# A two-layer hybrid block: attention scores of two heads at a time, the low-key part in the upper and lower half of the array

## The chip, the core and the metric

One core of a Trainium2 chip runs the whole program. Its tensor engine (PE) multiplies a stationary tile of weights (up to 128 rows by 128 columns) with a moving tile of up to 512 columns and adds into PSUM; the vector engine (DVE), the scalar engine (ACT) and GpSimd (POOL) do the rest, and sixteen DMA engines move data. Each engine works through its own instructions in the order in which they stand. The metric is the device time in microseconds, as the median of the runs.

## The reference, cut to what matters

Two layers of a hybrid backbone work on 512 latent tokens and 256 context tokens, 1024 channels wide. One input projection feeds four mixers: A global attention, W windowed attention, a spatial gating, an mLSTM; gates, a merge and an output projection follow. Both attentions have 8 query heads on 2 key/value heads, 64 channels a head. What the change touches is this part:

```python
def attend_dense(q, k, v):                                   # A: all 768 keys for a latent query
    s = jnp.einsum('bqhgd,bkhd->bhgqk', q, k).astype(jnp.float32) * HEAD_DIM ** -0.5
    p = jax.nn.softmax(s, axis=-1).astype(v.dtype)
    return jnp.einsum('bhgqk,bkhd->bqhgd', p, v)
...
    s_ctx = jnp.einsum('bqhgd,bkhd->bhgqk', qb, kc) * scale   # W: 256 context keys,
    s_loc = jnp.einsum('bqhgd,bkhd->bhgqk', qb, kb) * scale   # and the keys within 128 positions
    s_loc = jnp.where(ok, s_loc, -jnp.inf)
    p = sink_softmax(jnp.concatenate([s_ctx, s_loc], axis=-1))
```

Context queries read only the 256 context keys, and only in the first layer.

## The kernel before, in words

Tokens lie in six tiles of 128: tiles 0 to 3 latent, 4 and 5 context. Nearly all products are made on a type that PE runs at one pass (fp32r); for precision an operand is split into a high and a low part, and a product of two split operands is made of three: high by high, high by low, low by high. These are the helper's products on line 244 (`mm`), and most of PE's work is such projections into the PSUM tiles named `d`. Transposes, and a few products in the gate arithmetic, run in plain float32.

For the attention a query head has 64 channels, so its high and low part fit together: `rotate` (line 543 on) lays a query head down as 64 high and 64 low channels, and each key head twice, once as high, high and once as low, low. `turn` (line 574) transposes these with PE, so that the parts lie along the array's 128 rows: high in the upper 64 rows, low in the lower. A pass of a query tile over the doubled high keys is thus (high + low) by high, and one over the doubled low keys (high + low) by low, both with 128 rows.

`attend_scores` takes one head and a pair of query tiles. For each tile it fills one PSUM buffer `s` (there are two) with the scores, in pieces of 512, 256 or 128 keys, each piece in two passes; DVE adds masks and finds the maximum, ACT makes the exponential with its sum. `attend_values` transposes the probabilities of the pair (line 858), ACT and DVE split them (lines 861 and 862), and PE multiplies them with the split values into the buffer `b`; the high and low halves are added at the end (lines 874 and 876). In the windowed attention the two tiles of a pair share most of their keys; a key tile that only one of them sees gives a product of 128 columns.

What sets the order: the attention, the gate arithmetic and the mLSTM form one generator (`mixers`), the input projections another (`fill`). `interleave` hands out steps of the two by credit: a step of attention is worth its estimated time by a factor `RATIO`, one factor for each layer and phase, and steps of projections are drawn as long as there is credit. `FILL_ORDER` lists the projection units; a unit named t is an early merge gate, which otherwise is computed in the merge. Steps of `mixers` have a higher priority, and the framework's scheduler then orders each engine's instructions by a modelled time, so an instruction whose buffer isn't free in the model is passed over for one that can go.

Of the kernel before, what the change touches and what calls it, by code (L numbers as in the profile page):

```python
# [10 lines left out]
F32R = mybir.dt.float32r  # L11
AF = mybir.ActivationFunctionType
# [7 lines left out]
XT = 4  # L20
# [8 lines left out]
def _in_units():  # L29
# [27 lines left out]

OFF = 250
PP_FROM = 3
RATIO = ((1.5, 1.3, 1.5), (1.2, 0.4, 1.5))  # L60
N2, N3 = 1, 1
LEAD = (4,6)
LAG = 26.0
# [3 lines left out]
SIDE_K = 1  # L67
AFTER = {(0, 6): "g_v0", (0, 7): "g_v1", (2, 0): "g_u0", (2, 3): "g_u1"}
FILL_ORDER = (
    "w_kv w_q0 gate0_0 m0 m1 a_q1 m2 m3 m_o0 gate0_1 w_q1 t0_2 m4 gate1_0 t2_3 gate1_1 gate2_0 t3_3 t0_0 t2_0 gate2_1 t1_1 t1_0 gate3_0 m_o1 m5 t0_3 t1_3 t2_1 t0_1 t3_1 gate3_1 t1_2",  # L70
    "a_q1 m0 w_kv gate0_0 w_q0 m1 m2 g_v0 m3 w_q1 t1_1 m4 m_o0 gate0_1 t1_2 g_v1 t3_0 t0_2 m_o1 gate1_0 m5 t2_2 t0_3 g_u0 g_u1 gate1_1 t3_2 t2_0 gate2_0 gate2_1 t3_3 gate3_0 t3_1 gate3_1 t0_1 t1_3")
FIRST1 = (("kv", 4), ("x", 1), ("q", 2), ("x", 1), ("kv", 9), ("w", 1), ("q", 9))
FIRST0 = (("kv", 3), ("q", 3), ("kv", 9), ("w", 1), ("q", 9))
# [8 lines left out]
def tile_hybrid_block(ctx, tc, A, out):  # L82
# [16 lines left out]
    def S():  # L99
        return ps_s.tile([128, 1024], F32, tag="s", name="s")  # L100
# [142 lines left out]
    def mm(o, l, r, start, stop):  # L243
        pe.matmul(o, l, r, start=start, stop=stop)  # L244
# [307 lines left out]
    def rotate(ear, nh, t, g, tabs, copies):  # L552

        e, a, r = ear
        shape = [128, nh, 64]
        ev, av = (z.rearrange("p (h d) -> p h d", h=nh) for z in (e, a))
        if r is not None:
            dve.tensor_mul(ev, ev, bc(r.rearrange("p (h o) -> p h o", o=1), shape))
        if t < XT:
            dve.tensor_mul(av, ev, bc(tabs[0][:, t:t + 1, :], shape))  # L560
            dve.tensor_mul(ev, ev, bc(tabs[1][:, t:t + 1, :], shape))
            dve.tensor_add(av[:, :, 0:32], av[:, :, 0:32], ev[:, :, 32:64])
            dve.tensor_add(av[:, :, 32:64], av[:, :, 32:64], ev[:, :, 0:32])
            ev, e = av, a
        elif g is not None:
            dve.tensor_mul(ev, ev, bc(g.rearrange("p (o d) -> p o d", o=1), shape))
        st = ST()
        sv = st.rearrange("p (h s d) -> p h s d", h=nh, s=2 * copies)
        f = e.rearrange("p (h o d) -> p h o d", h=nh, o=1).to_broadcast([128, nh, copies, 64])
        act.copy(sv[:, :, 0:copies, :].bitcast(F32R), f)  # L570
        dve.tensor_sub(sv[:, :, copies:, :].bitcast(F32R), f, sv[:, :, 0:copies, :])
        return st

    def turn(st, dst, mark, done):
# [206 lines left out]
            act.activation(v[:, gs], ps[:, gs], AF.Identity, bias=sgb[:, g:g + 1])  # L781


    def attend_scores(qT, kv, kT, hl, pair, mode, sc, sink, sums):
        is_x = pair[0] < XT
        Ps = []
        for t in pair:
            ps = S()
            qs = qT[:, hl, t * 128:(t + 1) * 128]

            if not is_x:
                pieces = [(0, 512, 256)]
                cols = {4: 0, 5: 128}
                n = 256
            elif mode == "A":
                pieces = [(0, 0, 512), (512, 512, 256)]
                cols = {j: 128 * j for j in range(6)}
                n = 768
            else:
                loc = [j for j in (t - 1, t, t + 1) if 0 <= j < XT]  # L800
                cols = {4: 0, 5: 128}
                for i, j in enumerate(loc):
                    cols[j] = 256 + 128 * i
                pieces = [(0, 512, 256), (256, loc[0] * 128, 256)]
                if len(loc) == 3:
                    pieces.append((512, loc[2] * 128, 128))
                n = 256 + 128 * len(loc)
            for (pc, kc, cn) in pieces:
                mm(ps[:, pc:pc + cn], qs, kT[:, 2 * kv, kc:kc + cn], True, False)
                mm(ps[:, pc:pc + cn], qs, kT[:, 2 * kv + 1, kc:kc + cn], False, True)  # L810
            if is_x and mode == "W":
                if len(loc) == 3:
                    mv = ps[:, 256:768].rearrange("p (a b) -> p a b", a=2)[:, :, 0:128]
                    dve.tensor_add(mv, mv, mask)
                elif loc[0] == t:
                    dve.tensor_add(ps[:, 384:512], ps[:, 384:512], mask[:, 1, :])
                else:
                    dve.tensor_add(ps[:, 256:384], ps[:, 256:384], mask[:, 0, :])
            mx, nm, sm = YX(1), YX(1), sums[:, t:t + 1]
            dve.reduce_max(out=mx, in_=ps[:, :n], axis=AX.X)  # L820
            if sink is None:
                dve.tensor_scalar(nm, mx, -sc, None, op0=ALU.mult)
            else:
                dve.tensor_scalar(nm, mx, -sc, sink[0], op0=ALU.mult, op1=ALU.min)  # L824
            P = M(n)
            act.activation(P, ps[:, :n], AF.Exp, bias=nm[:, 0:1], scale=sc, accum_out=sm)  # L826
            if sink is not None:
                es = YX(1)
                act.activation(es, sink[1], AF.Exp, bias=nm[:, 0:1])
                dve.tensor_add(sm, sm, es)  # L830
            Ps.append((P, cols))
            yield 0.0011 * n
        return Ps

    def attend_values(Ps, Vt, kv, pair, mode, yT, hl):
        is_x = pair[0] < XT

        if not is_x:
            groups = [[(4, 0, 2), (5, 0, 2)]]
        elif mode == "A":  # L840
            groups = [[(j, 0, 2) for j in range(3)], [(j, 0, 2) for j in range(3, 6)]]
        else:
            c0, c1 = Ps[0][1], Ps[1][1]
            both = [j for j in range(XT) if j in c0 and j in c1]
            single = [(j, 0, 1) for j in range(XT) if j in c0 and j not in c1]
            single += [(j, 1, 1) for j in range(XT) if j in c1 and j not in c0]
            groups = [[(4, 0, 2), (5, 0, 2)] + single, [(j, 0, 2) for j in both]]
        pv = B()
        done = 0
        total = sum(len(g) for g in groups)  # L850
        for g in groups:
            n = sum(b[2] for b in g) * 128
            pt = S()
            o = 0
            for (j, q0, nq) in g:
                for qi in range(q0, q0 + nq):
                    P, cols = Ps[qi]
                    pe.transpose(pt[:, o:o + 128], P[:, cols[j]:cols[j] + 128], ident)  # L858
                    o += 128
            ph, pl = M(n, F32R), M(n, F32R)  # L860
            act.copy(ph, pt[:, :n])  # L861
            dve.tensor_sub(pl, pt[:, :n], rd(ph))  # L862
            o = 0
            for (j, q0, nq) in g:
                oc = slice(q0 * 128, (q0 + nq) * 128)
                ic = slice(o, o + nq * 128)
                vs = Vt[:, j, kv, :]
                mm(pv[:, oc], vs, ph[:, ic], done == 0, False)
                done += 1
                mm(pv[:, oc], vs, pl[:, ic], False, done == total)  # L870
                o += nq * 128
            yield 0.0017 * n
        tmp = XS(64)
        act.copy(tmp, pv[64:128, :256])
        o = 64 * (hl % 2)
        dve.tensor_add(yT[o:o + 64, :], pv[:64, :256], tmp)
        yield 0.0

    def attention(l, mode, b, ydram, rsd, res):
        nq = NT if l == 0 else XT  # L880
        sums = G48(8 * nq).rearrange("p (h t) -> p h t", h=8)
        pairs = [(0, 1), (2, 3)] + ([(4, 5)] if l == 0 else [])
        sc = 0.125
        if mode == "W":
            sk = const.tile([128, 16], F32, tag="sink", name="sink")
# [3 lines left out]
        for kv in range(2):  # L889
            yield ("need", (mode, kv))  # L890
            kT, Vt, qs = res[mode]
            for hp in range(2):
                for pair in pairs:
                    yT = XS()
                    for hl in (2 * hp, 2 * hp + 1):
                        h = 4 * kv + hl
                        sink = (sk[:, 8 + h:9 + h], sk[:, h:h + 1]) if mode == "W" else None
                        Ps = yield from attend_scores(qs[kv], kv, kT, hl, pair, mode, sc, sink, sums[:, h, :])
                        if pend is not None:
                            yield from finish_attend(pend, ydram, b, mode)  # L900
                        pend = (Ps, Vt, kv, pair, yT, hl, hp)
            if kv == 1:
                yield from finish_attend(pend, ydram, b, mode)
            release(res, "big", 1 + kv)
            release(res, "v6", kv)

# [8 lines left out]
    def finish_attend(pend, ydram, b, mode):  # L915
        Ps, Vt, kv, pair, yT, hl, hp = pend
        yield from attend_values(Ps, Vt, kv, pair, mode, yT, hl)
        if hl % 2 == 1:
            sy.dma_start(out=ydram[b, 2 * kv + hp][:, pair[0] * 128:pair[0] * 128 + 256], in_=yT)


    KAPPA = 0.25 * 128.0 ** -0.5
# [766 lines left out]
```

## Time and profile before

| | us |
|---|---|
| median of 3 runs | 2027.65 (2026.71 to 2029.03) |
| the profiled execution | 2029.01, of it span of the trace 2027.2 |
| PE busy in the span | 1983.9 |
| DVE, ACT busy | 1314.6, 972.7 |

The clock that TensorE was granted was 0.997 of full over the span. A start in the timeline is that of the operands' stream; the duration beside it is longer than the distance to the next start, since products overlap. So PE's pace is read from starts that follow each other.

### The profile page before, as it was taken

To read this page: it belongs to the slowest core of one execution; us is meant where nothing else is said; L and a number is where in the kernel's file an instruction comes from. 1 tells how busy PE (TensorE), PEld (TensorE's weight loads), DVE (VectorE), ACT (ScalarE), POOL (GpSimd) and SP (SyncE) were. 2 spreads that over 40 slices of the span, in tenths; PEclk is the share of its full clock that TensorE was granted. 3 is DMA by queue.
4 is the path that set the end of the run, shared out by engine and by line. 5 is a ranking of instruction groups with operands and counts; after the bars stand their busy time and mean duration, and the time that the engine had idled before them with its cause. 6 is when DMAs were issued, how large, how long until landed. Compare 5 with 4: busy or idle time off the path is not lost. (4 is left out here: it accounts for less than half of the span.)

```text
span 2027.2 us, 34553 instructions
## 1 busy us (share of the span) xinstructions
PE 1983.9 (98%) x13216; PEld 1805.3 (89%) x13216; DVE 1314.6 (65%) x2859; ACT 972.7 (48%) x2178; POOL 77.9 (4%) x88
## 2 busy tenths in 40 slices
PE   7999999999999999999999989999999999999998
PEld 5998998999999899999988989989989898888788
DVE  5766865676656766667445588667676565456765
ACT  5655554354544544334333466555555465443333
POOL 1200100000000000001000022000000000000000
PEclk9999999999999999999999999999999999999999
DMA  8112233333332544675343342223334335447745
GB/s 306 54 56 79 89 95 120 123 101 120 123 115 95 187 146 165 208 216 163 103 149 122 126 156 76 89 91 115 97 116 138 116 102 168 162 140 231 228 160 182
DMA packets 124271, 274.96 MB, mean 136 GB/s; under 512 B 16033, under 2 KB 41289, under 8 KB 123465
## 3 DMA queue, kind: packets, MB, share of 16 engines
q1 hardware_dynamic: 123560, 272.13, 40.9%
q8 instruction: 104, 1.70, 0.3%
q14 instruction: 63, 0.51, 0.1%
q0 software_dynamic: 256, 0.54, 0.1%
q10 hardware_dynamic: 288, 0.07, 0.0%
HBM read 219.33 MB, written 53.36 MB: 135 GB/s over the span
## 5 line engine op out<-in xcount | busy, mean ns | idle before, releaser
L244 PE MATMUL d<-xh,wh 128*128 128x512 f32 (+1 forms) x1504 | 536.6, 357 | 0.2
L244 PE MATMUL d<-xh,wl 128*128 128x512 f32 (+1 forms) x1504 | 534.4, 355 | 0.0
L244 PE MATMUL d<-xl,wh 128*128 128x512 f32 (+1 forms) x1504 | 533.5, 355 | 0.0
L228 DVE TENSOR_TENSOR wl<-wr,wh 128x1024 fp32r<-128x1024 f32 (+3 forms) x264 | 281.9, 1091 | 59.6 <-ACT wh L227 57.9
L244 PEld LDWEIGHTS d<-xh,wh 128*128 128x128 f32 x1504 | 284.3, 189 | 35.2 <-DVE st L686 0.3
L244 PEld LDWEIGHTS d<-xh,wl 128*128 128x128 f32 x1504 | 284.2, 189 | 34.7
L244 PEld LDWEIGHTS d<-xl,wh 128*128 128x128 f32 x1504 | 284.3, 189 | 33.8
L227 ACT CAST wh<-wr 128x1024 fp32r<-128x1024 f32 (+3 forms) x264 | 238.2, 946 | 138.4 <-PE s L244 52.8
L244 PE MATMUL d<-wh,xh 128*128 128x256 f32 (+1 forms) x976 | 282.8, 291 | 3.6 <-DVE xh L1567 1.9
L244 PE MATMUL d<-wh,xl 128*128 128x256 f32 (+1 forms) x976 | 278.5, 286 | 0.6 <-DVE xl L421 0.5
L244 PE MATMUL d<-wl,xh 128*128 128x256 f32 (+1 forms) x976 | 278.2, 286 | 0.8 <-DVE wl L228 0.8
L244 PEld LDWEIGHTS d<-wh,xh 128*128 128x128 f32 x976 | 186.6, 192 | 8.0 <-issue 4.5
L244 PEld LDWEIGHTS d<-wl,xh 128*128 128x128 f32 x976 | 187.2, 192 | 1.3 <-DVE wl L228 1.0
L244 PEld LDWEIGHTS d<-wh,xl 128*128 128x128 f32 x976 | 186.9, 192 | 1.4 <-DVE xl L421 0.9
L862 DVE TENSOR_TENSOR m<-s,m 128x768 fp32r<-128x768 f32 (+2 forms) x144 | 119.7, 837 | 97.7 <-ACT m L861 97.2
L244 PE MATMUL s<-big,wh 128*128 128x512 f32 (+1 forms) x656 | 163.8, 357 | 6.1 <-ACT big L1384 2.6
L826 ACT ACTIVATE m<-s,yx 128x768 f32<-128x768 f32 (+3 forms) x160 | 120.4, 753 | 96.8 <-DVE yx L824 49.4
L820 DVE TENSOR_REDUCE yx<-s 128x1 f32<-128x768 f32 (+3 forms) x160 | 122.4, 765 | 33.3 <-PE s L244 32.1
L861 ACT CAST m<-s 128x768 fp32r<-128x768 f32 (+2 forms) x144 | 100.9, 706 | 85.5 <-PE s L858 84.4
L244 PE MATMUL b<-m,v 128*128 128x256 f32 (+1 forms) x768 | 131.4, 284 | 2.9 <-DVE m L862 1.8
L244 PEld LDWEIGHTS s<-big,wh 128*128 128x128 f32 x656 | 107.3, 188 | 26.1 <-ACT big L1384 4.7
L244 PE MATMUL s<-big 128*128 128x256 f32 (+2 forms) x680 | 118.9, 302 | 0.7 <-ACT big L578 0.7
(343 smaller groups left out, 3064.6 us busy)
## 6 DMA issues: line engine op xcount, KB each, us to landing
wr<-in_w_in_dram SPq DMA_DIRECT2D x100, 512.0 KB, 4.2
wr<-in_w_mg_dram SPq DMA_DIRECT2D x50, 512.0 KB, 4.6
wr<-in_w_mod_dram SPq DMA_DIRECT2D x32, 512.0 KB, 4.6
wr<-in_w_out_dram SPq DMA_DIRECT2D x32, 512.0 KB, 4.6
th<-st SPq DMA_DIRECT2D x50, 256.0 KB, 2.4
wr<-in_w_bp_dram SPq DMA_DIRECT2D x50, 256.0 KB, 3.6
wr<-in_w_br_dram SPq DMA_DIRECT2D x28, 384.0 KB, 4.0
m<-th SPq DMA_DIRECT2D x26, 384.0 KB, 5.5
```

Of the source, the lines that this page charges most:

```text
L227: act.copy(wh[:, sl], raw)
L228: dve.tensor_sub(wl[:, sl], raw, rd(wh[:, sl]))
L244: pe.matmul(o, l, r, start=start, stop=stop)
L820: dve.reduce_max(out=mx, in_=ps[:, :n], axis=AX.X)
L826: act.activation(P, ps[:, :n], AF.Exp, bias=nm[:, 0:1], scale=sc, accum_out=sm)
L861: act.copy(ph, pt[:, :n])
L862: dve.tensor_sub(pl, pt[:, :n], rd(ph))
```

## The change

Scores are now made for two heads of one query tile, instead of for two tiles of one head. A query head's parts are laid down as high, low for the first head of a pair and low, high for the second, so that the high parts of the two heads lie in different halves of the rows. The pass over the high keys is as before. The pass over the low keys takes the high query part alone, with 64 rows: the first head in the upper half of the array, the second in the lower half, written in turns; low by low is left out. Context tiles keep 128 rows in both passes. The windowed pieces are laid out anew, so that the first is always 512 keys wide. The values follow with the two heads of a tile in 256 columns. Two of the ratios are lower, and the unit t3_2 of the first layer is computed early.

```diff
-RATIO = ((1.5, 1.3, 1.5), (1.2, 0.4, 1.5))
+RATIO = ((1.4, 1.2, 1.5), (1.2, 0.4, 1.5))
...
-    "w_kv w_q0 gate0_0 m0 m1 a_q1 m2 m3 m_o0 gate0_1 w_q1 t0_2 m4 gate1_0 t2_3 gate1_1 gate2_0 t3_3 t0_0 t2_0 gate2_1 t1_1 t1_0 gate3_0 m_o1 m5 t0_3 t1_3 t2_1 t0_1 t3_1 gate3_1 t1_2",
+    "w_kv w_q0 gate0_0 m0 m1 a_q1 m2 m3 m_o0 gate0_1 w_q1 t0_2 m4 gate1_0 t2_3 gate1_1 gate2_0 t3_3 t0_0 t2_0 gate2_1 t1_1 t1_0 gate3_0 m_o1 m5 t0_3 t1_3 t2_1 t0_1 t3_1 gate3_1 t1_2 t3_2",
...
-        sv = st.rearrange("p (h s d) -> p h s d", h=nh, s=2 * copies)
-        f = e.rearrange("p (h o d) -> p h o d", h=nh, o=1).to_broadcast([128, nh, copies, 64])
-        act.copy(sv[:, :, 0:copies, :].bitcast(F32R), f)
-        dve.tensor_sub(sv[:, :, copies:, :].bitcast(F32R), f, sv[:, :, 0:copies, :])
+        sv = st.rearrange("p (a s d) -> p a s d", a=2, s=4)
+        if copies == 2:
+            f = e.rearrange("p (h o d) -> p h o d", h=2, o=1).to_broadcast([128, 2, 2, 64])
+            hi, lo = sv[:, :, 0:2, :], sv[:, :, 2:4, :]
+        else:
+            f = e.rearrange("p (a b d) -> p a b d", a=2, b=2)
+            hi, lo = sv[:, :, 0::3, :], sv[:, :, 1:3, :]
+        act.copy(hi.bitcast(F32R), f)
+        dve.tensor_sub(lo.bitcast(F32R), f, hi)
...
+    def attend_scores(qT, kv, kT, hp, t, mode, sc, sinks, sums):
+        if t >= XT:
+            pieces = [(0, 256, slice(512, 768))]
+            cols = {4: 0, 5: 128}
+        elif mode == "A":
+            pieces = [(0, 512, slice(0, 512)), (512, 256, slice(512, 768))]
+            cols = {j: 128 * j for j in range(6)}
+        else:
+            first = (0, 1) if t < 2 else (2, 3)
+            cols = {first[0]: 0, first[1]: 128, 4: 256, 5: 384}
+            pieces = [(0, 512, None if t < 2 else slice(256, 768))]
+            if t in (1, 2):
+                cols[3 - t] = 512
+                pieces.append((512, 128, slice(384 - 128 * t, 512 - 128 * t)))
...
+        def products(ps, q, rows, kr, first):
+            for (pc, cn, ks) in pieces:
+                out, keys = ps[:, pc:pc + cn], kT[rows, kr, :]
+                if ks is None:
+                    mm(v3(out, 2), q, v3(keys, 3)[:, 0::2, :], first, not first)
+                else:
+                    mm(out, q, keys[:, ks], first, not first)
+                yield
+
+        qs = [qT[:, 2 * hp + i, t * 128:(t + 1) * 128] for i in range(2)]
+        pss = [S(), S()]
+        for i in range(2):
+            for _ in products(pss[i], qs[i], slice(0, 128), 2 * kv, True):
+                pass
+        rows = [slice(0, 128)] * 2 if t >= XT else [slice(0, 64), slice(64, 128)]
+        halves = [products(pss[i], qs[i][rows[i]], rows[i], 2 * kv + 1, False) for i in range(2)]
+        for _ in zip(*halves):
+            pass
...
+            if t < XT and mode == "W":
+                for j in (t - 1, t + 1):
+                    if j in cols and j < XT:
+                        mv = ps[:, cols[j]:cols[j] + 128]
+                        dve.tensor_add(mv, mv, mask[:, int(j > t), :])
...
+        keys = sorted(cols, key=lambda j: cols[j])
+        groups = [keys] if len(keys) == 2 else [keys[:3], keys[3:]]
...
-        o = 64 * (hl % 2)
-        dve.tensor_add(yT[o:o + 64, :], pv[:64, :256], tmp)
+        for i in range(2):
+            cs = slice(128 * i, 128 * i + 128)
+            dve.tensor_add(yT[64 * i:64 * i + 64, o:o + 128], pv[:64, cs], tmp[:, cs])
```

The order of PE's instructions at three places. The names: `s` with a number is a score buffer, so one number is one head and tile; `d` is a projection, `b` the values. First the start of global attention in the first layer, before, where one head and tile fills a buffer (two passes of 512, two of 256):

```order
L244 MATMUL d_1090<-wh_879,xl_129 128x256
L244 MATMUL s_1213<-big_590,big_643 128x512 x2
L244 MATMUL s_1213<-big_590,big_643 128x256 x2
L577 MATMUL d_1115<-ident_98,st_1021 128x128 x4
L244 MATMUL d_1134<-wh_879,xh_128 128x256
```

The same place in the changed program; the last four score products are the two heads' half products:

```order
L244 MATMUL d_1090<-wh_879,xh_128 128x256
L244 MATMUL d_1090<-wl_880,xh_128 128x256
L244 MATMUL s_1213<-big_590,big_643 128x512
L244 MATMUL s_1213<-big_590,big_643 128x256
L244 MATMUL s_1214<-big_590,big_643 128x512
L244 MATMUL s_1214<-big_590,big_643 128x256
L244 MATMUL s_1213<-big_590,big_643 128x512
L244 MATMUL s_1214<-big_590,big_643 128x512
L244 MATMUL s_1213<-big_590,big_643 128x256
L244 MATMUL s_1214<-big_590,big_643 128x256
L582 MATMUL d_1115<-ident_98,st_1021 128x128 x4
```

Here the second head's products have moved up to the first's, and the half products of the two stand in turns. The next query tile, before:

```order
L244 MATMUL d_1173<-wh_879,xh_128 128x256
L244 MATMUL s_1235<-big_590,big_643 128x512 x2
L244 MATMUL s_1235<-big_590,big_643 128x256 x2
L244 MATMUL d_1173<-wl_880,xh_128 128x256
L244 MATMUL d_1173<-wh_879,xl_129 128x256
```

And in the changed program, from the first head's last half products to the second head's:

```order
L244 MATMUL s_1235<-big_590,big_643 128x512
L244 MATMUL s_1235<-big_590,big_643 128x256
L244 MATMUL d_1173<-wl_880,xh_128 128x256
L244 MATMUL d_1173<-wh_879,xl_129 128x256
L244 MATMUL d_1173<-wh_879,xh_128 128x256
L244 MATMUL d_1173<-wl_880,xh_128 128x256
L244 MATMUL d_1173<-wh_879,xl_129 128x256
L244 MATMUL d_1173<-wh_879,xh_128 128x256
L244 MATMUL d_1173<-wl_880,xh_128 128x256
L244 MATMUL d_1173<-wh_879,xl_129 128x256
L244 MATMUL d_1173<-wh_879,xh_128 128x256
L244 MATMUL d_1173<-wl_880,xh_128 128x256
```

Ten projection products stand between the two heads, and the second head's four come behind them. Third, windowed attention of the first layer, before, two query tiles of one head:

```order
L244 MATMUL b_4493<-m_4500,v_1035 128x128
L244 MATMUL b_4493<-m_4501,v_1035 128x128
L244 MATMUL s_4573<-big_1034,big_1449 128x256 x4
L244 MATMUL s_4573<-big_1034,big_1449 128x128 x2
L244 MATMUL s_4590<-big_1034,big_1449 128x256 x4
```

In the changed program, two heads of one tile:

```order
L244 MATMUL s_4451<-big_1034,big_1450 128x512
L244 MATMUL s_4451<-big_1034,big_1450 128x128
L244 MATMUL s_4451<-big_1034,big_1450 128x512
L244 MATMUL s_4451<-big_1034,big_1450 128x128
L244 MATMUL d_5643<-wl_5402,xh_128 128x256
L244 MATMUL d_5643<-wh_5401,xl_129 128x256
L244 MATMUL s_4452<-big_1034,big_1450 128x512
L244 MATMUL s_4452<-big_1034,big_1450 128x128
L244 MATMUL s_4452<-big_1034,big_1450 128x512
L244 MATMUL s_4452<-big_1034,big_1450 128x128
```

Two pieces of 256 have become one of 512, and two projection products stand between the heads.

## Rows read from the trace of the kernel before

**Rows 1.** The page's head: busy us, share of the span, instructions; the largest DMA queue.

```profile
PE 1983.9 (98%) x13216; PEld 1805.3 (89%) x13216; DVE 1314.6 (65%) x2859; ACT 972.7 (48%) x2178; POOL 77.9 (4%) x88
...
q1 hardware_dynamic: 123560, 272.13, 40.9%
```

**Rows 2.** Busy time by stretches: stretch, length, each engine's busy us.

```profile
500.00:700.00 200.00, 200.00 (x1336) 183.28 (x1335) 127.51 (x297) 97.94 (x234) 0.00 (x0) 1.00 0.38 123
```

**Rows 3.** Waits of PE: total us, times, longest.

```profile
PE b L244 <- DVE m L862: 1.8, 1, 1.8
```

**Rows 4.** Timeline of PE, global attention: start us, us, instruction.

```profile
151.62 0.86 PE L244 MATMUL s<-big 128*128 128x512 f32 x4
152.31 0.39 PE L244 MATMUL d<-xl,wh 128*128 128x512 f32 x1
```

**Rows 5.** Timeline of PE, windowed attention.

```profile
432.13 1.40 PE L244 MATMUL s<-big 128*128 128x256 f32 x10
433.37 0.64 PE L244 MATMUL b<-m,v 128*128 128x256 f32 x4
```

**Rows 6.** Timeline of PE, transposes of the split type.

```profile
438.40 0.46 PE L577 MATMUL d<-ident,st 128*128 128x128 f32 x4
438.69 0.35 PE L244 MATMUL d<-xh,wh 128*128 128x256 f32 x1
```

**Rows 7.** Timeline of PE, five float32 transposes and the second product behind.

```profile
440.92 0.71 PE L858 MATMUL s<-ident,m 128*128 128x128 f32 x5
...
441.58 0.28 PE L244 MATMUL d<-xl,wh 128*128 128x256 f32 x1
```

**Rows 8.** Timeline of PE, 64-row products, first layer (64*128 is rows*columns).

```profile
412.77 0.28 PE L244 MATMUL d<-wh,xl 128*128 128x256 f32 x1
412.98 0.43 PE L244 MATMUL b<-g,ones 64*128 64x64 f32 x2
413.25 0.22 PE L982 MATMUL b<-ident,gcb 64*128 64x64 f32 x1
413.40 0.39 PE L244 MATMUL d<-wh,xh 128*128 128x256 f32 x1
413.62 0.28 PE L244 MATMUL d<-wl,xh 128*128 128x256 f32 x1
```

**Rows 9.** Timeline of PE, the same three products in the second layer.

```profile
1489.08 0.39 PE L244 MATMUL d<-xl,wh 128*128 128x512 f32 x1
...
1490.16 0.40 PE L244 MATMUL d<-xh,wh 128*128 128x512 f32 x1
```

**Rows 10.** Timeline of PE, six small float32 products with 128 rows.

```profile
398.41 0.28 PE L244 MATMUL d<-xh,wl 128*128 128x256 f32 x1
398.53 0.52 PE L244 MATMUL b<-g,tri 128*128 128x24 f32 x4
398.89 0.40 PE L244 MATMUL b<-g,ones 128*128 128x48 f32 x2
...
399.31 0.28 PE L244 MATMUL d<-xl,wh 128*128 128x256 f32 x1
```

**Rows 11.** Timeline of PE, a group of 32-column products in the prologue.

```profile
28.76 0.29 PE L244 MATMUL d<-wh,xl 128*128 128x272 f32 x1
28.98 1.07 PE L244 MATMUL s<-wh,xs 128*32 128x256 f32 x16
29.98 0.40 PE L244 MATMUL d<-wh,xh 128*128 128x272 f32 x1
30.21 0.29 PE L244 MATMUL d<-wl,xh 128*128 128x272 f32 x1
```

**Rows 12.** Groups by line and form: busy us, mean ns, idle before.

```profile
L820 DVE TENSOR_REDUCE yx<-s 128x1 f32<-128x768 f32 x64 | 60.9, 952 | 15.3 <-PE s L244 14.9
L876 DVE TENSOR_TENSOR xs<-b,xs 64x256 f32<-64x256 f32 x80 | 33.2, 415 | 31.8 <-ACT xs L874 30.5
...
L816 DVE TENSOR_TENSOR s<-s,mask 128x128 f32<-128x128 f32 x16 | 4.7, 295 | 8.0 <-PE s L244 7.9
...
L826 ACT ACTIVATE m<-s,yx 128x768 f32<-128x768 f32 x64 | 57.8, 903 | 43.0 <-DVE yx L822 41.0 <-PE s L858 1.6
```

More of the change, by code (lines that the diff above doesn't have):

```diff
@@ L781, in spatial_mix @@
             act.activation(v[:, gs], ps[:, gs], AF.Identity, bias=sgb[:, g:g + 1])
-    def attend_scores(qT, kv, kT, hl, pair, mode, sc, sink, sums):
-        is_x = pair[0] < XT
-        Ps = []
[L787 to L819, printed above, removed]
@@ new lines, in attend_scores @@
+    def attend_scores(qT, kv, kT, hp, t, mode, sc, sinks, sums):
[12 more added lines that the diff above has]
+                pieces.append((512, 128, slice(384 - 128 * t, 512 - 128 * t)))
+        n = 128 * len(cols)
+        def products(ps, q, rows, kr, first):
[15 more added lines that the diff above has]
+            pass
+        Ps = []
+        for i, ps in enumerate(pss):
+            if t < XT and mode == "W":
[3 more added lines that the diff above has]
+                        dve.tensor_add(mv, mv, mask[:, int(j > t), :])
+            mx, nm, sm = YX(1), YX(1), sums[:, i, t:t + 1]
@@ L820, in attend_scores @@
             dve.reduce_max(out=mx, in_=ps[:, :n], axis=AX.X)
-            if sink is None:
+            if sinks is None:
                 dve.tensor_scalar(nm, mx, -sc, None, op0=ALU.mult)
             else:
-                dve.tensor_scalar(nm, mx, -sc, sink[0], op0=ALU.mult, op1=ALU.min)
+                dve.tensor_scalar(nm, mx, -sc, sinks[i][0], op0=ALU.mult, op1=ALU.min)
             P = M(n)
             act.activation(P, ps[:, :n], AF.Exp, bias=nm[:, 0:1], scale=sc, accum_out=sm)
-            if sink is not None:
+            if sinks is not None:
@@ L828, in attend_scores @@
                 es = YX(1)
-                act.activation(es, sink[1], AF.Exp, bias=nm[:, 0:1])
+                act.activation(es, sinks[i][1], AF.Exp, bias=nm[:, 0:1])
                 dve.tensor_add(sm, sm, es)
-            Ps.append((P, cols))
+            Ps.append(P)
             yield 0.0011 * n
[L833 to L847, printed above, removed]
+        return Ps, cols
@@ L848, in attend_values @@
+    def attend_values(Ps, cols, Vt, kv, yT, o):
+        keys = sorted(cols, key=lambda j: cols[j])
+        groups = [keys] if len(keys) == 2 else [keys[:3], keys[3:]]
         pv = B()
         done = 0
-        total = sum(len(g) for g in groups)
         for g in groups:
-            n = sum(b[2] for b in g) * 128
+            n = len(g) * 256
             pt = S()
[L854 to L859, printed above, removed]
+            for i, (j, P) in enumerate((j, P) for j in g for P in Ps):
+                pe.transpose(pt[:, i * 128:i * 128 + 128], P[:, cols[j]:cols[j] + 128], ident)
@@ L862, in attend_values @@
             dve.tensor_sub(pl, pt[:, :n], rd(ph))
[L863 to L866, printed above, removed]
+            for i, j in enumerate(g):
+                ic = slice(i * 256, i * 256 + 256)
                 vs = Vt[:, j, kv, :]
-                mm(pv[:, oc], vs, ph[:, ic], done == 0, False)
+                mm(pv[:, :256], vs, ph[:, ic], done == 0, False)
                 done += 1
-                mm(pv[:, oc], vs, pl[:, ic], False, done == total)
-                o += nq * 128
+                mm(pv[:, :256], vs, pl[:, ic], False, done == len(keys))
             yield 0.0017 * n
@@ L881, in attention @@
         sums = G48(8 * nq).rearrange("p (h t) -> p h t", h=8)
-        pairs = [(0, 1), (2, 3)] + ([(4, 5)] if l == 0 else [])
         sc = 0.125
@@ L892, in attention @@
             for hp in range(2):
[L893 to L901, printed above, removed]
+                h = 4 * kv + 2 * hp
+                sinks = [(sk[:, 8 + h + i:9 + h + i], sk[:, h + i:h + i + 1]) for i in range(2)] if mode == "W" else None
+                for t in range(nq):
+                    if t % 2 == 0:
+                        yT = XS()
+                    Ps, cols = yield from attend_scores(qs[kv], kv, kT, hp, t, mode, sc, sinks, sums[:, h:h + 2, :])
+                    if pend is not None:
+                        yield from finish_attend(pend, ydram, b)
+                    pend = (Ps, cols, Vt, kv, t, yT, hp)
             if kv == 1:
-                yield from finish_attend(pend, ydram, b, mode)
+                yield from finish_attend(pend, ydram, b)
             release(res, "big", 1 + kv)
@@ L913, in attention, with finish_attend @@
         sy.dma_start(out=rsd[b].rearrange("h (t q) -> (h t) q", q=128), in_=rows[:8 * nq, :])
[L915 to L919, printed above, removed]
+    def finish_attend(pend, ydram, b):
+        Ps, cols, Vt, kv, t, yT, hp = pend
+        yield from attend_values(Ps, cols, Vt, kv, yT, 128 * (t % 2))
+        if t % 2 == 1:
+            sy.dma_start(out=ydram[b, 2 * kv + hp][:, t * 128 - 128:t * 128 + 128], in_=yT)
     KAPPA = 0.25 * 128.0 ** -0.5
```

## The prediction

> **What bounds the kernel now.** I read the page's head first. TensorE (PE) is busy 98% of the span, the vector engine (DVE) 65%, the scalar engine (ACT) 48%, and the DMA queue's packets take about 41% of the engines' time [rows 1]. The table by stretches then says what that means in the attention: from 500 to 700 us, where the first layer's windowed attention stands beside the projections, PE is busy all 200 us, DVE 127.5 and ACT 97.9 [rows 2]. The list of waits agrees: the longest total that PE waits for anything of the attention's softmax, the split of the probabilities, is 1.8 us in the whole span [rows 3]. So the time is the time that PE's own queue takes. Work on the other engines is worth nothing as long as it stays under PE, and each nanosecond that PE's stream gains or loses in the attention is one of the total.
>
> PE's pace comes from starts that follow each other, not from the mean durations, since the products overlap. Four score products (two of 512 columns, two of 256) start at 151.62 and the next starts at 152.31: 0.69 us, so 0.227 for 512 and 0.12 for 256 [rows 4]. Ten score products of 256 in the windowed attention take 1.24 us, 0.12 each [rows 5]. Four transposes of 128 columns on the split type take 438.40 to 438.69, 0.07 each; I use 0.065 for any 128-column product of that type [rows 6]. A 128-column float32 transpose costs (441.58 - 440.92 - 0.12) / 5 = 0.11 [rows 7].
>
> **What leaves.** (a) Low-key products. Each head and tile of latent queries makes two passes, over the high and the low part of the keys, both with 128 rows [rows 4, 5]. After the change the low pass uses 64 rows, upper half for one head, lower half for the other, and two of them can share the time of one where they follow each other directly. The order of the changed program decides how often that is. Of its 224 half products, in 120 unbroken runs, most stand with one head alone: 48 runs are "512, 256" of one head, 34 a single 512, 15 "512, 128" of one head. Only 14 runs hold a 512 of both heads, 6 of those a pair of 256 too. The scheduler put the second head behind its own buffer, with other products between (the pieces from the order show one pair kept together and two that were parted). The gain is 14 x 0.227 = 3.2 us and 6 x 0.12 = 0.7; the few pairs of 128 columns I put at nothing, since two loads of weights stand in the time of each. Sum -3.9 us.
> (b) Windowed scores are cut 512 + 128 or 512 in place of 256 + 256 (+ 128). 64 head-tiles in two passes, each 2 x 0.12 - 0.23 = 0.01: -1.3 us.
> (c) Windowed values: by the two orders 64 products of 128 columns go and 32 of 256 come: -64 x 0.065 + 32 x 0.12 = -0.3 us. Every other PE product is in both programs equally often; the moved unit t3_2 and the ratios only change places.
>
> **What comes.** (d) Entering and leaving the 64-row form. The old kernel does it twice, in the gate arithmetic, where three small float32 products read 64 rows. From the last full product before to the second behind: 412.77 to 413.62 = 0.85 us, where 2 x 0.12 + 3 x 0.11 = 0.57 is work: 0.28 lost [rows 8]. Second layer: 1489.08 to 1490.16 = 1.08, work 2 x 0.227 + 3 x 0.11 = 0.78: 0.30 lost [rows 9]. It is not small float32 products as such: six of those with all 128 rows, in the same arithmetic, lie between 398.41 and 399.31 = 0.90 with 2 x 0.12 + 6 x 0.11 = 0.90 of work, nothing lost [rows 10]. It isn't rows alone either: in the prologue a group of 32-column products starts 0.22 after a product of 272 columns, whose pace is 0.12 x 272 / 256 = 0.13 [rows 5], and behind the group the second such product comes 0.23 after the first: 0.09 + 0.10, some 0.20 with the rounding, is lost [rows 11]. So a visit costs 0.20 to 0.30. The product that enters there loads float32 weights; its transposes pace at 0.11 against 0.065 of the split type, so I take 0.045 off the middle of 0.28 and 0.30, and use 0.24. Nothing hides it: PE waits for no one there. 120 x 0.24 = +28.8 us; ends 120 x 0.20 = 24 and 120 x 0.30 = 36. Below 0.20 speaks only that no row shows a 512-column product of this type entering; that is a rival below.
>
> The Trainium skill, TensorEngine Tiling (Array Packing), section Tiling Modes, says that a change of tiling mode, unlike a change of tile, drains the engine; it has no price, and the trace has its price [rows 8, 9, 11]. The Trainium skill, TensorE: Matmul & The Clock Gate, Part 3, adds a rule against this change: weights load beside a running product only where the row group differs. For full products the trace shows the contrary: 256 columns every 0.12 us, each with weights of its own, so the load is hidden [rows 5]. Were it so inside the 64-row form, the 63 second products of one head would each show a load, and an estimate with 0.065 a load [rows 6] is 4 us more; I leave it out of the sum.
>
> (e) Hidden at nothing. DVE gains 80 additions (the last one of a unit in two halves, 0.295 each by the nearest row in place of 0.415) and 32 of masks (two narrow ones for one wide, put at a whole 0.295): 80 x 0.175 + 32 x 0.295 = 23 us at most [rows 12], spread over the attention, in which DVE is a third idle [rows 2]; without that cover it would be up to 23. The unit t3_2 is done early: its tanh goes out to memory and comes back, and its weights come by two loads; the queue has room at 41% [rows 1]. New waits: a pair wants both score buffers at once, and all projections queue behind it on PE. PE's waits for ACT and DVE are small and I cost this at nothing, but keep it as a rival.
>
> **The sum.** -3.9 - 1.3 - 0.3 + 28.8 = +23.3 us on the profiled execution's 2029.0 us (span 2027.2), which is 1.4 us above the median of the runs; on the median, 2027.65 + 23.3 = 2051. Its own range by the ends of (d): 2046 to 2058.
>
> **Rivals.**
> 1. *The visit is free for wide products.* Entering and leaving hide under the 512 columns that run before and in the visit. For: the visits in the trace have small or float32 products only [rows 8, 9, 11]. Against: in both, part of the loss is at the first wide products behind. Then only (a) to (c) are left: 2027.65 - 5.5 = 2022, faster.
> 2. *Most halves share the array anyway*, as the change says. 64 pairs at 0.227 and 32 more of 256 at 0.12 would be 18.4, with free visits 2027.65 - 18.4 - 1.6 = 2008. Against: products run in the order of the queue, and there the second head's half mostly stands behind full products.
> 3. *The pairs wait for the second score buffer* on top of my sum. One reduction and one exponential, 0.95 + 0.90 us, stand between a buffer and its release [rows 12]; at 14 pairs 26 us: 2077. It decides if PE reaches the pair within 1.9 us of the earlier buffer's last product. Against: the waits of that kind are short now [rows 3].
> 4. *A cheap visit*, about 0.05 us: 120 x 0.05 - 5.5 = +0.5, no change. Against: none is below 0.20 [rows 8, 9, 11].
>
> **How the numbers follow.** My forecast 0.76, rival 1 0.11, rival 2 0.03, rival 3 0.05, rival 4 0.05. 0.2% is 4.1 us, about what a measurement of this kernel can tell from no change. Slower: forecast and rival 3, 0.81; within: rival 4, 0.05, and 0.01 from the edge of rival 1; faster: the rest, 0.13. Slower begins at a visit of (5.5 + 4.1) / 120 = 0.08 us. For 8 in 10 the range goes from a visit of 0.08 (2032) to my upper end with a quarter of rival 3's waits, 6 us, on top (2064).
>
> **What would show it.** In the profile after: single half products with 0.1 us or so more before them and before the next full one, and PE's busy share still 98%; pairs of 512 whose starts lie a few ns apart; 224 half products of 64 rows; 32 windowed value products more of 256 and none of 128; and no new row at the head of PE's waits. I am wrong if the start after a lone half product comes 0.227 behind it and the one after that on pace, or if PE idles for the buffers of the scores.

## The result, and the profile after

The changed kernel takes 2071.98 us (median of 4 runs, 2067.94 to 2077.44) against 2027.66 (2026.71 to 2029.03): a ratio of 1.0216, with a 95% interval of 1.0204 to 1.0228. That is +44.3 us, where +23.3 was forecast; the direction was right, the size about half, and the time lies above the range.

The head of the page after, to be read against [rows 1]; the columns are busy time, share of the span, instructions.

```profile
span 2069.2 us, 34406 instructions
...
PE 2019.0 (98%) x13056; PEld 1788.5 (86%) x13056; DVE 1330.5 (64%) x2971; ACT 971.5 (47%) x2178; POOL 75.3 (4%) x88
```

PE makes 160 products fewer and is busy 35.1 us longer; it is idle for 50.2 us of the span where it was 43.3. So the loss is mostly inside PE's own stream. PEld's busy time fell from 1805.3 to 1788.5 us: there isn't more loading either. The waits of PE after, in total, times and longest:

```profile
PE b L244 <- DVE xs L164: 7.2, 1, 7.2
PE s L406 <- DVE big L403: 4.4, 5, 1.7
...
PE s L858 <- ACT m L840: 2.8, 2, 2.2
```

The first two belong to the prologue. The wait for the exponential (last row) stands at 2.8 us; no wait is large enough for 44 us.

Now one half product's visit. The timeline of PE after, global attention, one head and tile (512 and 256 columns with 128 rows, then 512 and 256 with 64 rows; the view puts the four in one row, named by the first):

```profile
94.26 0.28 PE L244 MATMUL d<-wh,xh 128*128 128x256 f32 x1
94.38 1.06 PE L244 MATMUL s<-big 128*128 128x512 f32 x4
95.36 0.39 PE L244 MATMUL d<-wl,xh 128*128 128x256 f32 x1
95.59 0.28 PE L244 MATMUL d<-wh,xl 128*128 128x256 f32 x1
```

In [rows 4] the same four take 0.69 us from the first start to the next product. Here it is 95.36 - 94.38 = 0.98, and the product behind takes another 0.23 where 0.12 is its pace: (0.98 - 0.69) + (0.23 - 0.12) = 0.40 lost. The loads in the same stretch say where it goes; the bracket is PEld's idle time before:

```profile
94.26 0.31 PEld L244 LDWEIGHTS s<-big 128*128 128x128 f32 x2
94.82 0.29 PEld L244 LDWEIGHTS s<-big 64*128 64x128 f32 x2 [0.25 <-issue]
95.36 0.19 PEld L244 LDWEIGHTS d<-wl,xh 128*128 128x128 f32 x1 [0.25 <-issue]
```

Elsewhere a product's weights load while the one before still runs, so PEld hardly rests. At both borders of the visit it stands still for 0.25 us, with nothing in the profile that it waits for. And there a load starts together with its product (94.82, 95.36), where elsewhere it starts 0.12 us before (94.26 for the product at 94.38). By the single starts the 0.39 to 0.40 us fall into four parts: 0.09 before the first half product, 0.11 behind it, 0.09 before the first full product and 0.10 behind that. The two parts behind are as long as a load that nothing covers, 0.11; what the array does in the two parts before, no run shows.

A pair of heads that the order kept together, from the second head's first product on (six products: its 512 and 256, then 512, 512, 256, 256 with 64 rows):

```profile
1343.85 1.06 PE L244 MATMUL s<-big 128*128 128x512 f32 x6
1344.83 0.38 PE L244 MATMUL d<-xh,wl 128*128 128x256 f32 x1
1345.05 0.28 PE L244 MATMUL d<-xh,wh 128*128 128x256 f32 x1
```

From the first start to the second product behind it is 1.20 us, as for the four above (95.59 - 94.38 = 1.21). The second head's halves cost nothing here: they do share the array. The groups by form show what became of the low-key pass:

```profile
L244 PE MATMUL s<-big 64*128 64x512 f32 x128 | 56.6, 496 | 0.0
...
L244 PE MATMUL s<-big 64*128 64x256 f32 x64 | 16.3, 280 | 0.0
...
L244 PE MATMUL s<-big 64*128 64x128 f32 x32 | 6.8, 238 | 0.0
```

These are the 224 half products of the forecast. For every visit one can take the distance from the last full product before to the second one behind, less the paces. Of the visits that hold one product or two of one head, and have no other visit right beside them, 88 of 92 cost 0.38 to 0.40 us, whichever they hold. All 120 together, less what pairs share, lose 42 us by the starts.

### The profile page after: what moved, and what is told of

Read it like the earlier page. It is cut to its first block, busy times and chain, and to the rows that moved or that the text cites. A ratio compares the mean times of both kernels' runs of the same rounds, so it can differ in the third digit from the quotient of the medians.

```text
span 2069.2 us, 34406 instructions
## 1 busy us (share of the span) xinstructions
PE 2019.0 (98%) x13056; PEld 1788.5 (86%) x13056; DVE 1330.5 (64%) x2971; ACT 971.5 (47%) x2178; POOL 75.3 (4%) x88
## 4 chain that ended last, share of the span: by engine, by line
PE 86%; DMA 5%; DVE 4%; ACT 2%; issue 1%; POOL 0%; SPq 0%; POOLq 0%; DVEq 0%; ACTq 0%
PE d L244 61%; PE s L244 13%; PE b L244 7%; PE s L858 4%; DMA m<-sg 2%; DMA m<-rs 2%; PE d L582 1%; DVE wl L228 1%; DVE m L1379 0%; ACT m L418 0%; ACT wh L227 0%; DMA big<-in_x_dram 0%; DVE m L1378 0%; POOL yd L326 0%; DMA wr<-in_w_bp_dram 0%
## 5 line engine op out<-in xcount | busy, mean ns | idle before, releaser
L244 PE MATMUL s<-big 64*128 64x512 f32 (+5 forms) x552 | 134.3, 352 | 1.1 <-DVE m L861 1.1
L244 PE MATMUL b<-m,v 128*128 128x256 f32 x736 | 133.5, 292 | 0.8 <-ACT m L860 0.8
```

## The experiments

Theory V after the result: each visit to the 64-row form costs about 0.39 us, whatever it holds, and that is the slowdown. Rivals: the new order of the work (R), a price as forecast, and later what the price depends on.

### 128 rows everywhere (e1)

```diff
-        rows = [slice(0, 128)] * 2 if t >= XT else [slice(0, 64), slice(64, 128)]
+        rows = [slice(0, 128)] * 2
```

> The changed kernel with 128 rows in the low-key pass too (so low by low is computed again); everything else of the change stays. Theory V (each visit to the 64-row form costs about 0.39 us, whatever it holds, less the time that two heads' half products share; that is all of the slowdown): no visits are left beside the two of the gate arithmetic, and what remains is the new cutting of windowed scores and values, -1.6 us: 2026 (2022 to 2030), no change. Rival R (the new order of the work is slower too: two score buffers taken together, other ratios, one early unit): the time stays above 2035.

2034.0 us (6 runs), ratio to before 1.003 (1.0018 to 1.0042). So by the medians of two groups of runs 38.0 of the 44.3 us hang on the 64-row form, and some 7 do not. The same place of the timeline as above:

```profile
94.27 0.88 PE L244 MATMUL s<-big 128*128 128x512 f32 x4
94.98 0.28 PE L244 MATMUL d<-wl,xh 128*128 128x256 f32 x1
95.10 0.28 PE L244 MATMUL d<-wh,xl 128*128 128x256 f32 x1
```

And the head of its page:

```profile
PE 1984.5 (97%) x13056; PEld 1799.0 (88%) x13056; DVE 1328.9 (65%) x2971; ACT 972.2 (48%) x2178; POOL 75.2 (4%) x88
```

The four products and the one behind now take 0.83 us where they took 1.21, and PE's busy time falls by 34.5 us. V's 2026 was missed, and so was R's "above 2035": the form is most of it, and R holds a small part.

### Halves of the two heads kept together (e2)

```diff
-            for _ in products(pss[i], qs[i], slice(0, 128), 2 * kv, True):
+            for full in products(pss[i], qs[i], slice(0, 128), 2 * kv, True):
                 pass
...
-        for _ in zip(*halves):
-            pass
+        with tc.issue_after(full.ins):
+            for _ in zip(*halves):
+                pass
```

> The changed kernel with the half products of both heads queued behind the last full product of the second head, so that they stand together: 72 visits instead of 120, 61 of them with a 512 of both heads. Theory V: 72 x 0.39 = +28.1 us, shared 61 x 0.227 + 32 x 0.12 + 12 x 0.065 = -18.5, cutting -1.6: +8.0 on before, 2036 (2031 to 2041), still slower than before. Rival P (pairs pay as the change says, a visit of 0.24 as I had forecast): 72 x 0.24 - 20.1 = -2.8: 2025. Rival R: near the changed kernel's 2072 less the shared 14.6 us, above 2050.

2097.65 us (4 runs), ratio 1.0346 (1.0332 to 1.036): slower than the change, and no theory's number. The visits themselves are as V says: by the starts, the 72 visits less what pairs share lose 10 us, where V has 28.1 - 18.5 = 9.6. Even the 31 visits that hold a pair of 512 and a pair of 256 lose 0.04 us each, and the 16 with a pair of 512 alone 0.16. The rest is new. Waits, and two stretches (length, busy us of PE, PEld, DVE, ACT, POOL, granted clock, DMA):

```profile
PE b L244 <- ACT xs L1106: 13.6, 4, 4.0
...
PE d L582 <- DVE st L576: 5.9, 2, 4.5
```

```profile
100.00:300.00 200.00, 191.66 (x1325) 174.32 (x1324) 131.59 (x281) 102.87 (x210) 6.24 (x6) 0.97 0.23 75
300.00:500.00 200.00, 200.00 (x1311) 179.58 (x1310) 125.77 (x320) 82.78 (x176) 0.00 (x0) 1.00 0.36 118
...
700.00:900.00 200.00, 185.26 (x1185) 165.33 (x1184) 120.08 (x325) 90.48 (x248) 3.97 (x3) 0.97 0.44 138
```

And three pieces of the first of them, by ten us:

```profile
220.00:230.00 10.00, 7.15 (x60) 6.72 (x59) 6.52 (x13) 5.17 (x11) 1.01 (x1) 1.00 0.18 57
230.00:240.00 10.00, 9.66 (x44) 7.87 (x42) 3.09 (x11) 3.06 (x8) 0.00 (x0) 0.83 0.19 63
240.00:250.00 10.00, 5.52 (x28) 5.49 (x28) 9.96 (x32) 3.41 (x8) 1.11 (x1) 0.70 0.06 17
```

PE idles 84.1 us (2096.1 less 2012.0 busy), 33 more than in e1, its waits add up to 75.7 us against 43.1 there, and the granted clock isn't full any more: behind the 2.9 us in which PE stood still (220 to 230) it is 0.83, and then 0.70. With two levels, 2.4 and 1.2 GHz, that is 3.4 and 6.0 of these ten us each at the lower one; in the stretch without idle time it is 1.00. By the starts of the products that run at the lower clock it costs 19 us over the span, against 4 in the changed kernel. The waits are not for score buffers: the longest is the mLSTM's (L1106), and all score products together wait for less than 4 us. Holding the first head's halves back until the second head's buffer is full moves everything behind them. So this run shows that forcing the pairs in this way costs more than it gives; the pairs themselves, as the starts above say, at best come out even.

### The old kernel with halves of one head (e4)

```diff
+            if is_x and mode == "A":
+                for (pc, kc, cn) in pieces:
+                    mm(ps[:, pc:pc + cn], qs, kT[:, 2 * kv, kc:kc + cn], True, False)
+                for (pc, kc, cn) in pieces:
+                    mm(ps[:, pc:pc + cn], qs[0:64], kT[0:64, 2 * kv + 1, kc:kc + cn], False, True)
+            else:
...
```

> The kernel before, with 64 rows (the high query part, always the upper half) in the low-key pass of global attention's latent queries alone; low by low is left out there. Nothing else of the change: one head at a time, the old buffers, ratios and units. 62 visits, and no two heads can share the array, since both would use the upper half. Theory V: 62 x 0.39 = +24: 2052 (2048 to 2056). A visit of 0.24 as forecast: +15: 2043. Rival R: no change, 2028.

2049.59 us (2 runs), ratio 1.0109 (1.0091 to 1.0128): +22.3, with nothing of the change but 62 visits. PE's busy time grows by 24.0 us to 2007.9, 0.39 a visit; its idle time shrinks by 3. By the starts the visits lose 23.9. The visit is a cause by itself, without the new order, and 0.24 (+15) is excluded.

```profile
94.61 1.06 PE L244 MATMUL s<-big 128*128 128x512 f32 x4
95.60 0.39 PE L244 MATMUL d<-wl,xh 128*128 128x256 f32 x1
95.82 0.28 PE L244 MATMUL d<-wh,xl 128*128 128x256 f32 x1
```

The stretch is 1.21 us again (95.82 - 94.61), as in the changed kernel. The head of this kernel's page, to be read against [rows 1], with the same instructions on every engine:

```profile
PE 2007.9 (98%) x13216; PEld 1805.4 (88%) x13216; DVE 1315.7 (64%) x2859; ACT 972.1 (47%) x2178; POOL 78.1 (4%) x88
```

### Halves cut into 128 columns (e5)

```diff
+        if mode == "A" and t < XT:
+            for c in range(0, 768, 128):
+                for i in range(2):
+                    mm(pss[i][:, c:c + 128], qs[i][rows[i]], kT[rows[i], 2 * kv + 1, c:c + 128], False, c in (384, 640))
+        else:
...
```

> The changed kernel with the half products of global attention cut into six of 128 columns per head. The scheduler puts other products between them, so there are 202 visits, 14 of them with six 128s of one head in a row and 5 with both heads' twelve in turns. Theory V: about 202 x 0.39 = 79 us of visits, 3 for the cutting, less 3 shared and 1.6: +77: 2105 (2095 to 2115); inside a visit of six, starts 0.06 apart, as for full products. Rival L (inside the 64-row form weights load only beside a product of other rows): in a run of six of one head each start comes 0.06 later still, about 0.12 apart, and in turns of two heads it does not.

2121.68 us (one run), +94 where V says +77. A run of six of one head, behind its 512 and 256:

```profile
94.11 0.28 PE L244 MATMUL d<-wh,xh 128*128 128x256 f32 x1
94.23 1.33 PE L244 MATMUL s<-big 128*128 128x512 f32 x8
95.49 0.39 PE L244 MATMUL d<-wl,xh 128*128 128x256 f32 x1
95.71 0.28 PE L244 MATMUL d<-wh,xl 128*128 128x256 f32 x1
```

1.48 us against 1.21 with two products: 0.27 more, of which 6 x 0.065 - 0.35 = 0.04 is the cutting as V reckoned it. The other 0.23 is that the starts inside lie 0.11 apart and not 0.065: 0.045 for each of five. With the heads in turns it is also 0.11, but for two products at once.

That looks like rival L, but it is not a property of the form. In the kernel before, with all 128 rows, two products of 128 columns that follow each other in the windowed scores:

```profile
422.25 0.34 PE L244 MATMUL s<-big 128*128 128x128 f32 x2
422.42 0.33 PE L244 MATMUL d<-wl,xh 128*128 128x256 f32 x1
422.59 0.28 PE L244 MATMUL d<-wh,xl 128*128 128x256 f32 x1
```

The two take 0.17 us (single starts: 0.06, then 0.11), and the wide product behind them 0.17 in place of 0.12. In that whole trace no two loads of 128 columns by this helper with all rows start closer than 0.108 us. So 0.065 holds for a product of 128 columns alone between wider ones, where its load is hidden; a row of them goes at the pace of the loads, 0.11, with all rows as with 64. What the form has of its own is that the two halves load at the same time: with the heads in turns two products go in each 0.11. Products of 256 columns and more hide the load in the form too: where e4's kernel made the halves of two query tiles in one visit (512, 512, 256, 256, all in the upper half), the visit costs 0.39 above the paces like any other.

By the starts all visits of this run lose 87 us, 8 more than V had for them, which is this pace; products at the lower clock (granted 0.990 over the span) cost another 8 above before.

### Visits of one small product (e7), and visits in float32 (e8)

```diff
+                if is_x and mode == "A" and pc == 512:
+                    cn = 192
+                    mm(ps[:, 704:768], qs[0:64], kT[0:64, 2 * kv + 1, 704:768], False, False)
```

> The kernel before, where of the low-key pass of global attention the last 64 of 768 keys are made by a product of 64 rows and 64 columns, standing alone between full products; the low-by-low part of these keys is left out. 62 visits of one small product. Theory V (0.39 us a visit whatever it holds, the load of the first product included): from the last full product before to the second behind 0.39 above their paces plus at most 0.03 for the 64 columns; time +24 to +26: 2052 (2049 to 2056). Rival S (small products make a cheap visit, 0.28 as I read from the gate arithmetic): +17 to +19: 2045.

2061.78 us (2 runs), ratio 1.0165 (1.0146 to 1.0183), above both. The visit, in a row that begins with the second 512: 512 and 256 with all rows, 64 columns with 64 rows, 192 with all rows:

```profile
88.08 1.02 PE L244 MATMUL s<-big 128*128 128x512 f32 x4
88.94 0.47 PE L577 MATMUL d<-ident,st 128*128 128x128 f32 x4
```

From the second 512 to the transposes 0.86 us; the paces of 512, 256 and 192 columns come to 0.23 + 0.12 + 0.09 = 0.44, so the one small product adds 0.42. Over its 60 single visits the starts give 0.41 to 0.42: 0.39 above the 0.03 that 64 columns stream. Rival S is out: a small visit isn't cheap. The visits lose 24 us by the starts, as V says; of the 8 us above that, the profiled run shows 4 as idle time of PE (47.4 us against 43.3) and 2 as products at the lower clock. Why the cut pass makes PE wait is not shown.

```diff
-                    mm(ps[:, pc:pc + cn], qs[0:64], kT[0:64, 2 * kv + 1, kc:kc + cn], False, True)
+                    mm(ps[:, pc:pc + cn], rd(qs[0:64]), rd(kT[0:64, 2 * kv + 1, kc:kc + cn]), False, True)
```

> The kernel before with 64 rows in the low-key pass of global attention as in e4, but these products in plain float32, two passes each. 64 visits; streaming grows by 64 x 0.35 = 22 us. Theory V: 64 x 0.39 + 22 = +47: 2075, and 0.39 in each visit above the doubled paces. Rival F (the type of the entering weights changes the price by 0.045, as I had taken it): 0.43 to 0.44 in each visit, 2078.

2111.71 us (one run), well above both, because a float32 product streams far slower than I had put it. The same place as above, 512 and 256 with all rows, then four passes in float32:

```profile
97.17 2.00 PE L244 MATMUL s<-big 128*128 128x512 f32 x6
99.10 0.38 PE L244 MATMUL d<-wh,xl 128*128 128x256 f32 x1
99.32 0.28 PE L244 MATMUL d<-wh,xh 128*128 128x256 f32 x1
```

The starts inside are 0.53, 0.43, 0.215 and 0.31 us apart, so the two passes of 512 stream in 0.43 each and those of 256 in 0.215. 2.15 us, less 0.23 + 0.12 + 2 x 0.43 + 2 x 0.215 + 0.12, leaves 0.39: the type doesn't matter, F is out. The extra streaming, 64 x (1.29 - 0.35) = 60 us, and 64 x 0.39 = 25 make the 84.

### What the other 7 us are (e6, e10, e11, e12)

The tables of the other code, the one early unit (t3_2) included; this is the edit of e6 on top of e1's, and e10 makes it the other way round on the old kernel:

```diff
-RATIO = ((1.4, 1.2, 1.5), (1.2, 0.4, 1.5))
+RATIO = ((1.5, 1.3, 1.5), (1.2, 0.4, 1.5))
```

> The 128-row variant of the change (e1) with the old tables: ratios 1.5 and 1.3 in the first layer, unit t3_2 back in the merge. e1 stood 6.7 us above before, with no visits. Theory T (the tables, made for another program, starve PE): back to 2026 to 2029. Theory L (scores of two heads at a time take both buffers and PE waits for them): stays at 2032 to 2036.

> The kernel before with the new tables (ratios 1.4 and 1.2, t3_2 early), nothing else. Theory T: 2032 to 2036. Theory L: 2026 to 2030.

With 128 rows, the changed code and the old tables: 2047.39 us, ratio 1.0092 (1.0079 to 1.0105). The old kernel with the new tables: 2034.28, ratio 1.0034 (1.0021 to 1.0047). So the old kernel stands where T put it, and the other run stands above both theories. Each code is better with its own tables: the new ones gain 13 us for the new code (2047.4 to 2034.0, over two groups of runs), so they are no cause of the 7, and T falls.

Then the score buffer of the second head was taken only behind the first head's softmax, as in the old kernel:

```diff
-        pss = [S(), S()]
...
-        for i, ps in enumerate(pss):
+        for i in range(2):
+            ps = S()
+            for first in (True, False):
+                for _ in products(ps, qs[i], slice(0, 128), 2 * kv + 1 - first, first):
+                    pass
```

> The 128-row variant of the change (e1, new tables), but each head's score buffer is taken and filled only after the first head's softmax is issued, as in the kernel before; values still for two heads of a tile. Theory L2 (e1's 7 us above before come from taking both score buffers at once): back to 2025 to 2029. Rival M (they come from the rest of the rearrangement: values of two heads, their groups, and an order that the tables meet less well): stays at 2032 to 2036.

> The same as e11 with the old tables (e6 stood at 2047). Theory L2: 2025 to 2030. Rival M: 2040 to 2048.

2028.77 us (11 runs), ratio 1.0011 (1.0002 to 1.002), and with the old tables 2040.53, ratio 1.0068 (1.0054 to 1.0082). Against the kernel before of the same group that is 2.0 us above in place of 6.7, and with the old tables 13.8 in place of 19.6. So about 5 of the 7 us go away when the buffers are taken one after the other (L2; the intervals of the two ratios leave room for 1 to 7); e12 itself stands where M put it, since the old tables cost 12 us on the new code in both forms. No variant is faster than the kernel before.

That PE waits for a score buffer is not shown. In e1 the score products are preceded by no idle time (0.0, the last number of the first row below; 0.0 too for the narrower ones). What could be such a wait, that of the transposes into `s` for the exponential, is longer in the faster kernel; the further rows are before, e1 and e11:

```profile
L244 PE MATMUL s<-big 128*128 128x512 f32 x256 | 89.1, 402 | 0.0
...
PE s L858 <- ACT m L826: 0.8, 1, 0.8
...
PE s L858 <- ACT m L840: 3.8, 2, 2.4
...
PE s L854 <- ACT m L836: 7.6, 4, 2.6
```

What differs is the order of everything: PE is idle 50.9 us in e1 and 46.9 in e11 (43.3 before), in waits all over the span.

## Why the prediction was wrong, step by step

**What bounds the kernel**: right. PE is at 98% before and after, and e1 and e4 move the time by about what they move PE's busy time (34.5 of 38.0, 24.0 for 22.3).

**(a) What the halves share**: right. 14 runs had a 512 of both heads, and there the second head is free; the pairs of 128, put at nothing, share 0.065 too. About -4.4 for -3.9.

**(b), (c) New cutting**: put too low. 0.065 was read from transposes [rows 6] and used for all 128-column products, but of the helper's products two in a row, with the delay behind them, take 0.22 us (e5). So the 64 value products that go, nearly all in pairs, are about 7 us and not 4.2, and (c) is about -3 in place of -0.3. In all, PE's products outside the visits take some 7 us less by the starts after the change than before, and 4 less in e1, where -1.6 was forecast. In the whole time this is covered by other things: e11, which has the new cutting and no visit, is 2 us above before.

**(d) The visit**: the step that failed. The mechanism and the count (120) were right, and so was the sign that I gave, some 0.1 us before a half product and before the next full one (0.09 each); the 0.11 behind the half product I had taken for its work. The price is 0.39 and not 0.24, 120 x 0.39 = 46.8 for 28.8, and the end of my range, 0.30, was too low as well. Two things went wrong in reading [rows 8, 9]. I took off 3 x 0.11 as the work of the three small products. But 0.11 is the pace of their loads, and the first load is just what the border exposes: with 2 x 0.11 the same rows give 0.85 - 0.24 - 0.22 = 0.39 and 1.08 - 0.45 - 0.22 = 0.41. Products that stream long would have shown it, and there were none. Then I took off 0.045 because those weights are float32; e8 shows that the type is nothing. The lower end, from [rows 11], took what shows before the group and behind the first wide product after it, and left out what shows in between: four rounds at 0.216 us by the single starts are 0.86 of the 1.00 us from 28.98 to 29.98, so 0.14 more.

**(e) Hidden at nothing**: right for DVE, whose extra additions stayed under PE. Wrong in putting the new order at nothing: PE is idle 7 us longer after than before. That is rival 3 only in part: taking both buffers at once is worth about 5 us (e1 against e11), but by no wait for a score buffer that a trace shows; after the change the score products wait for 1.1 us in all. Where the pairs were forced (e2), PE's idle time grew most, and there too the waits are others'.

By the terms as measured, in the two profiled runs, whose spans are 42.0 us apart: 46.8 - 4.4 = 42.4 for the visits less the pairs, +7 of idle time, -7 for PE's other products and -1 at the lower clock, together 41. The idle time, put at nothing, and the cutting, put at -1.6, were both mis-sized and cancel, which is luck. Of the 21 us that the forecast missed, the price of the visit makes 18. By the medians it is 38.0 for the form and 6.7 for the order. That 38.0 is less than 42 is in part e1's lower clock (0.994 over the span against 0.997: 9 us of its products' time against 4); the rest stays open.

**The rivals**: 1 (free for wide products) and 4 (cheap) fall by e4, where wide products alone cost 0.39 a visit. 2 was decided by the order: 14 of 64 possible pairs met.

**What the Trainium skill says**: The Trainium skill, TensorEngine Tiling (Array Packing), section Tiling Modes, names a drain of the engine at a change of mode. The trace agrees that a change costs time for which no wait is named, and puts in and out together at 0.39 us; that a drain is what fills the 0.09 before the first product at each border is not shown. At the measured price the change would not pay with all pairs either: a visit of one pair shares 0.35 us at most in global attention (0.23 + 0.12) and 0.23 to 0.29 in windowed, each below 0.39, and the visits of e2 bear it out. By the same rows a visit would have to hold two pairs or more to gain, as an estimate; no run tried that.

The Trainium skill, TensorE: Matmul & The Clock Gate, Part 3, lets a load overlap a running product only where the row group differs. The measurements say otherwise for these products: behind products of 256 columns and more of the same rows no load shows, with all rows [rows 5] or inside the form (e4), and the 0.11 of short products is the same in both. So for this change it was right to leave that rule out of the sum.

## What to carry to other kernels

Count the visits to another array form in the order that the scheduler makes, not the products that could share it; here each visit in and out costs 0.39 us of a stream that nothing else bounds, and one pair of 512 columns gives back 0.23. When a price is read from a stretch of small products, subtract only what the stretch would take without the cost that one looks for: a pace of 0.11 that is set by loads is no work where the first load is part of the cost. And a pace read from one kind of short product (0.065, transposes) need not hold for a row of another (0.11). A tuned table belongs to the code it was tuned for: the old code lost 7 us with the new tables, the new code with 128 rows 13 with the old.

## What the runs showed of the hardware that was not expected

A change between the 128-row and the 64-row form shows half of its price before the product and half behind it, where the first load in the other form is not hidden: 0.09 and 0.11 going in, 0.09 and 0.10 coming out. Loads of 128 columns for the helper's products never start closer together than 0.108 us with all rows (the kernel before), and go at 0.11 in the form; there the two halves load at the same time (e5). A float32 pass of 512 columns streams in 0.43 us in the form, and a product takes two: 3.8 times the 0.227 of the split type (e8). At a border PEld rests 0.25 us without a wait that the profile names; what the array does before the product starts no run here shows.
